# Query, key and value projections of a padded attention kernel as 64-row matmul pairs in two phases

## The chip, the cores and the metric

The kernel runs on one core of a Trainium2 chip. The metric is the device time in microseconds (us) of one execution, from its start to its end. Three executions were timed; their median is the number that a change is compared with.

## What is computed

32 sequences of up to 512 rows of 512 numbers are given with their lengths. For each sequence the rows within its length are projected to queries, keys and values of 8 heads with 64 columns each, and softmax attention over those rows is computed. Rows past the length are zero in the output.

```python
batch, max_seq, n_heads, head_dim = (32, 512, 8, 64)
for b in range(batch):
    seq_len = lengths[b]
    x_b = x[b, :seq_len].copy()
    qkv = np.matmul(x_b, w_qkv)
    q, k, v = np.split(qkv, 3, axis=-1)
    ...
    scores = scale * np.matmul(q, k.transpose(0, 2, 1))
    scores_max = np.max(scores, axis=-1, keepdims=True)
    attn = np.exp(scores - scores_max)
    attn = attn / (np.sum(attn, axis=-1, keepdims=True) + 1e-08)
    out_b = np.matmul(attn, v).transpose(1, 0, 2).reshape(seq_len, dim)
    output[b, :seq_len] = out_b
```

The lengths of this draw, sorted, are 502 447 | 446 436 | 363 357 | 351 347 | 343 333 | 323 315 | 310 261 | 260 257 | 246 230 | 223 220 | 216 183 | 164 152 | 143 140 | 134 119 | 101 86 | 79 75.

## The kernel before

A part ahead of the loops sorts the sequences by length on the chip, loads the weights and makes the projections of the longest sequence. Then the sequences are worked on in pairs, longest first. There is a loop for each width N of 512, 448, 384, 352, 320, 288, 256, 224, 192, 160, 128 and 96 columns, and a pair runs in the narrowest loop that holds it. For this draw the loops 512, 448 and 384 run once, 352 three times, 320, 288 and 256 once, 224 twice, 192 once, 160 twice, 128 and 96 once. N up to 512 and 448 means n = 4 tiles of 128 rows, 384 to 288 means n = 3, and 256 to 160 n = 2.

A loop's body has two positions, one for each sequence of the pair. A position does the attention of its own sequence and makes the projections of the next one, from `xT`, the transposed input. What it does in which order is written by hand as a string of steps in the table `ORDER`; two strings with a bar between them are for the first and the second position, one string is for both. A step is emitted on all engines that take part in it, and every engine keeps to the order of its own instructions. The steps that matter here:

- `Q0` to `Q3`, `K0` to `K3`: one 128-column block of queries or keys, 4 matmuls with 128 rows and N columns (line 261) into one PSUM bank, and a copy of the bank to `qz` or `kT` (line 1202). `V0` to `V3`: the values of one tile of rows, 4 matmuls with 128 rows and 512 columns (line 272), and a copy to `v_aug` (line 1218). A star puts the copy on ACT, else it is on DVE. `W0` makes the last values of both sequences of a pair at once (line 1109) where they fill at most half of the last tile.
- `S0`, `S1` and so on: scores. In loops of 3 and 4 tiles a step is two matmuls with 64 rows and N columns, one for each head of a pair of heads (line 1155), into two banks, and one exponential on ACT from both banks (line 1173).
- `A0` and so on: attention times values of one head (4 tiles, 16 matmuls with 65 columns) or two heads (3 tiles, 18 matmuls), line 1244, into one bank. Three DVE instructions follow: the reciprocal R of the row sums (line 1254), its product U with a mask (line 1260) and the division O into the output tile (line 1263), which frees the bank.
- `L`, `P`, `D`, `X` are the mask columns, the casts of the next input on POOL, the loads, and the transposing DMA that fills `xT` for the position after the next, which SP issues when the last projection that reads that `xT` is done.

There are 8 PSUM banks. `allotted` (line 945) gives each step the bank that has been free longest, and scores two neighbouring banks. `plan_waits` (line 36) derives from each step's reads and writes the semaphore waits of every instruction; a matmul into a bank waits for the copy, exponential or division that read it last. Between instructions of PE there is no wait.

## Time and profile before

| what | value |
| --- | --- |
| median of the runs | 338.09 us (337.75 to 338.3, 3 runs) |
| span of the profiled execution | 336.7 us |
| PE busy | 322.2 us (96%), 3832 matmuls |
| ACT busy | 264.5 us (79%) |
| DVE busy | 210.0 us (62%) |
| POOL busy | 103.6 us (31%) |

For the profiled execution only its span is known, from the first to the last instruction; the runs' median is 1.4 us above it. PE is the engine of the matmuls, PEld its weight loads, which overlap them; DVE and ACT are the two engines that read the banks; SP issues the DMAs. Matmuls are pipelined, so that the busy time of PE does not tell whether it is at its peak; the starts of successive matmuls do. In a timeline row stand the start in the span, the time from the first start to the last end, the engine, the line, the operation, its form (rows\*columns of the weights, then the moving operand) and how many instructions were merged.

### The profile page before, as it was taken

The numbers are of one execution on the slowest core, as the hardware profiler recorded it, in microseconds if no ns is written. First come the engines' busy times: TensorE is split into PE (matmuls) and PEld (weight loads), VectorE is DVE, ScalarE is ACT, GpSimd is POOL, SyncE is SP. The second block draws the span as 40 slices with busy tenths as digits, with TensorE's granted clock in tenths as the row PEclk, the third lists the DMA queues.
The fourth block names the chain that finished last, engine by engine and source line by source line (L and its number), as shares of the span: only waits on it lengthen the run. The fifth ranks groups of instructions, "written<-read, shape, count | busy, mean of one in ns | idle before, by whom it ended". The sixth has DMA issues, their size and how long they took to land.

```text
span 336.7 us, 10690 instructions
## 1 busy us (share of the span) xinstructions
PE 322.2 (96%) x3832; PEld 200.0 (59%) x3832; DVE 210.0 (62%) x654; ACT 264.5 (79%) x416; POOL 103.6 (31%) x149
## 2 busy tenths in 40 slices
PE   7999999999999999999999999999999999999881
PEld 4444545554555556556556656665677777678760
DVE  6676666666666564465455457665776656867764
ACT  5388799898978879989989988788567678777651
POOL 5546040504030320330231253043222244244321
PEclk9999999999999999999999999999999999999998
DMA  6974994484637946957947848969946966977671
GB/s 218 391 270 108 324 177 145 121 305 116 207 51 237 318 142 228 288 173 277 300 140 275 239 140 321 258 173 341 262 139 182 204 193 169 207 229 210 219 196 71
DMA packets 72124, 72.08 MB, mean 214 GB/s; under 512 B 41872, under 2 KB 41872, under 8 KB 72080
## 3 DMA queue, kind: packets, MB, share of 16 engines
q1 hardware_dynamic: 72032, 71.52, 71.9%
q8 instruction: 24, 0.39, 0.5%
q14 instruction: 20, 0.16, 0.2%
q10 hardware_dynamic: 48, 0.00, 0.0%
HBM read 28.32 MB, written 33.55 MB: 184 GB/s over the span
## 4 chain that ended last, share of the span: by engine, by line
PE 91%; DVE 3%; DMA 3%; issue 1%; SPq 0%; POOL 0%; ACT 0%; POOLq 0%
PE banks L261 38%; PE banks L272 18%; PE banks L1244 17%; PE banks L1155 16%; PE banks L1109 2%; DMA xT<-x 1%; DMA x_nat<-in_x_dram 1%; DVE out_nat L1263 1%; DVE rcp L1260 1%; PE banks L732 0%; DVE rcp L1254 0%; SPq L609 0%; DVE kT L781 0%; ACT et L1173 0%; DVE x L327 0%
## 5 line engine op out<-in xcount | busy, mean ns | idle before, releaser
L1173 ACT ACTIVATE et<-banks 128x704 f16<-128x704 f32 (+7 forms) x260 | 195.6, 826 | 31.7 <-PE banks L1155 30.3
L261 PE MATMUL banks<-xT,w_r 128*128 128x352 f16 (+11 forms) x1024 | 145.5, 287 | 1.4 <-DMA xT<-x 1.2
L332 POOL TENSOR_TENSOR x<-x_nat,mask 128x512 f16<-128x512 f32 x85 | 86.2, 1039 | 182.9 <-DVE mask L998 170.7
L261 PEld LDWEIGHTS banks<-xT,w_r 128*128 128x128 f16 x1024 | 85.4, 98 | 41.8 <-issue 7.4
L1244 PEld LDWEIGHTS banks<-v_aug,et 128*128 128x128 f16 x1792 | 66.4, 98 | 21.3 <-issue 7.2
L1244 PE MATMUL banks<-v_aug,et 128*128 128x65 f16 x1792 | 74.2, 194 | 0.7 <-ACT et L1173 0.7
L272 PE MATMUL banks<-w_r,xT 128*128 128x512 f16 x284 | 72.3, 380 | 0.6 <-DVE xT L741 0.5
L1263 DVE TENSOR_TENSOR out_nat<-banks,rcp 128x256 f32<-128x256 f32 (+1 forms) x136 | 64.1, 472 | 6.8 <-DMA out_dram<-out_nat 2.2
L1155 PE MATMUL banks<-qz,kT 64*128 64x352 f16 (+11 forms) x640 | 61.2, 298 | 2.9 <-DVE out_nat L1263 2.5
L1254 DVE RECIPROCAL rcp<-banks 128x4 f32<-128x4 f32 (+1 forms) x136 | 25.0, 184 | 44.3 <-PE banks L1244 42.8
L1202 DVE CAST qz<-banks 128x352 f16<-128x352 f32 (+5 forms) x44 | 25.3, 575 | 26.3 <-PE banks L261 25.8
L1155 PEld LDWEIGHTS banks<-qz,kT 64*128 64x128 f16 x640 | 22.6, 94 | 31.8 <-issue 23.4
L272 PEld LDWEIGHTS banks<-w_r,xT 128*128 128x128 f16 x284 | 23.7, 97 | 27.2 <-issue 5.2
L1218 DVE CAST v_aug<-banks 128x512 f16<-128x512 f32 x41 | 28.2, 692 | 16.7 <-PE banks L272 16.6
L1202 ACT CAST kT<-banks 128x352 f16<-128x352 f32 (+5 forms) x58 | 27.6, 478 | 10.2 <-PE banks L261 9.0
L1202 ACT CAST qz<-banks 128x352 f16<-128x352 f32 (+5 forms) x47 | 22.2, 477 | 6.0 <-PE banks L261 4.3
L1202 DVE CAST kT<-banks 128x512 f16<-128x512 f32 (+4 forms) x33 | 19.4, 590 | 7.3 <-PE banks L261 6.9
L1260 DVE TENSOR_TENSOR rcp<-rcp,v_aug 128x4 f32<-128x4 f32 (+1 forms) x108 | 19.6, 181 | 3.7
L1218 ACT CAST v_aug<-banks 128x512 f16<-128x512 f32 x26 | 15.6, 602 | 6.6 <-PE banks L272 6.6
L1074 DVE TENSOR_SCALAR v_aug<-alive 128x24 f16 (+3 forms) x32 | 7.7, 239 | 6.5 <-issue 6.5
L1341 POOL MEMSET kT<- 128x128 f16 (+1 forms) x8 | 1.7, 218 | 28.8 <-PE banks L1155 28.8
L418 PE MATMUL banks<-h_ones 128*128 128x128 f16 (+2 forms) x34 | 5.7, 349 | 1.9 <-POOL h_ones L408 1.9
(81 smaller groups left out, 84.0 us busy)
## 6 DMA issues: line engine op xcount, KB each, us to landing
x_nat<-in_x_dram SPq DMA_DIRECT2D x12, 768.0 KB, 5.5
out_dram<-out_nat SPq DMA_DIRECT2D x12, 768.0 KB, 4.0
x_nat<-in_x_dram SPq DMA_DIRECT2D x14, 512.0 KB, 3.8
x_nat<-in_x_dram SPq DMA_DIRECT2D x7, 1024.0 KB, 6.9
out_dram<-zeros SPq DMA_DIRECT2D x12, 512.0 KB, 5.6
out_dram<-out_nat SPq DMA_DIRECT2D x12, 512.0 KB, 4.5
out_dram<-out_nat SPq DMA_DIRECT2D x4, 1024.0 KB, 4.9
out_dram<-zeros SPq DMA_DIRECT2D x12, 256.0 KB, 5.5
```

Of the source, the lines that this page charges most:

```text
L261: last = nc.tensor.matmul(dst[:, 0:N], w_r[:, c, w0 : w0 + P], xT[:, c, 0:N], start=(c == 0), stop=(c == NC - 1),)
L272: last = nc.tensor.matmul(pv, xT[:, c, t * P : (t + 1) * P], w_r[:, c, 2 * D : 3 * D], start=(c == 0), stop=(c == NC - 1),)
L332: return engine.tensor_tensor(out=x16, in0=x32, in1=live.broadcast_to([P, D]), op=ALU.mult)
L1074: return nc.vector.tensor_scalar(out=v_bufs[o][:, t0:t1, :, HD], in0=table[:, bass.ds(at("DVE") + (j + 1), 1), t0:t1] .rearrange("p o t -> ...
L1155: last = nc.tensor.matmul(psc[par][:, x * wide : x * wide + N], kT[r, i, c0 : c0 + P], qz[r, i, 0:N], start=True, stop=True,)
L1173: return nc.scalar.activation(out=et[:, :, x0:x1, 0:N], in_=got.rearrange("p j (x q) -> p j x q", q=wide)[:, :, x0:x1, 0:N], func=AF.Exp, ...
L1202: return copy_on(act)(out=buf[:, ms, 0:N], in_=bank[:, 0 : gm * N].rearrange("p (m q) -> p m q", q=N),)
L1218: return copy_on(act)(out=v_bufs[o][:, t, :, 0:HD], in_=bank.rearrange("p (h d) -> p h d", d=HD))
L1244: last = nc.tensor.matmul(pav[:, g, qt, :], e_bufs[e][:, c0 + qt * P : c0 + (qt + 1) * P], v_aug[:, kt, h, :], start=(kt == 0), stop=(kt = ...
L1254: return nc.vector.reciprocal(out=rcp, in_=pav[:, :, :, HD])
L1260: return nc.vector.tensor_tensor(out=rcp, in0=rcp, in1=rows, op=ALU.mult)
L1263: return nc.vector.tensor_tensor(out=o_t[:, 0:n, h0 * HD : (h0 + heads) * HD].rearrange("p t (g d) -> p g t d", d=HD), in0=pav[:, :, :, 0:HD],
```

## The change

In loops of 3 and 4 tiles the steps Q, K and most of V are replaced by steps in two phases. `B0a` is the first phase and `B0b` the second of the queries' and keys' block 0; `U0a` and `U0b` are those of the values of tiles 0 and 1. A phase is four pairs of matmuls with 64 rows each, one on rows 0 to 63 and one on rows 64 to 127. In the first phase the upper rows' products go to one bank and the lower rows' to the other, in the second phase the banks are exchanged, so that both banks then hold complete sums. The second phase waits on PE's own semaphore for the last matmul of the first (`after`). The letters behind the colon say which engine copies each of the two banks, d for DVE and a for ACT. The digits behind @ give the banks of each step of these loops by hand, in place of `allotted`. All strings of these loops are new, the letters L, P, D and X included; those of the loops of 2 tiles and of 1 are the same. Some last matmuls of the A steps raise semaphores of steps that a loop doesn't have (`pads`).

```diff
@@ -31,6 +31,8 @@
     writes: tuple = ()
     dma: bool = False
     skip: bool = False
+    after: str = ""
+    pads: tuple = ()
 
 
 def plan_waits(head, bodies, entries, rare):
@@ -104,6 +106,8 @@
                     for o, is_read in needs
                     if o["by"] != op.eng or op.dma or (is_read and op.eng != "PE")
                 ]
+                if op.after:
+                    needs.append(seen[op.after][-1])
                 for o in sorted(needs, key=lambda o: -o["order"]):
                     if mine[o["by"]] >= o["count"]:
                         continue
@@ -216,28 +220,38 @@
     LOOPS = [512, 448, *range(384, 64, -32)]
 
     ORDER = {
-        512: "L P D S0 S1 S2 V2 K3 Q2 S3 S4 S5 Q3 V1 S6 K2 S7 S8 A0 S9 A1 V3* A2 S10 S11 S12 A3 K0 "
-        "Q1 A4 S13 S14 S15 V0 Q0* A5 K1* X A6 A7",
-        448: "L P D S0 S1 S2 K1 Q3 K3 S3 S4 Q2 S5 S6 V1 A0 S7 A1 S8 S9 V0 Q0 S10 S11 S12 A2 A3 V2* "
-        "A4 S13 S14 S15 K0* A5 K2* Q1 X A6 A7 | L P D S0 S1 V2 S2 S3 V1 K3 S4 S5 S6 K2 Q0 W0* S7 "
-        "S8 S9 K0 A0 Q1* A1 S10 S11 S12 A2 A3 K1* Q2 S13 S14 S15 A4 V0 A5 Q3* X A6 A7",
-        384: "L P D K1* Q1 S0 S1 S2 Q3 Q2* V1 S3 S4 V2 S5 S6 V0 A0 S7 S8 K0 Q0 S9 S10 S11 A2 K2* "
-        "A4 K3* X A6 | L P D S0 S1 S2 V0* Q0 Q3 S3 S4 S5 A0 V1 V2* S6 S7 S8 A2 K1 K3* Q1 S9 S10 "
-        "S11 A4 K2 K0 Q2* X A6",
-        352: "L P D S0 S1 S2 V0 K0* V1 S3 S4 S5 A0 V2* K1* S6 S7 S8 A2 Q2 K3* Q1* S9 S10 S11 Q0 A4 "
-        "Q3* K2* X A6",
-        320: "L P D S0 S1 S2 K0* Q2 Q1* S3 S4 S5 A0 K1 Q0* K3 S6 S7 S8 V1 V0 S9 S10 S11 A2 A4 Q3* "
-        "K2* X A6 | L P S0 S1 S2 W0* D Q1 Q2 Q3 S3 S4 S5 V1 Q0* A0 S6 S7 K2* V0 S8 S9 S10 K0 A2 A4 "
-        "S11 K3* K1 X A6",
-        288: "L P D S0 S1 V0 S2 S3 K3 K2* Q0* S4 S5 S6 A0 K1 Q2* K0 S7 S8 S9 A2 V1 S10 S11 A4 Q3* "
-        "Q1* X A6 | L P S0 S1 S2 V0 W0 D S3 S4 S5 V1 K2 Q1* K1* S6 S7 S8 A0 K0* Q0* K3* S9 S10 S11 "
-        "Q3 A2 Q2* X A4 A6",
+        512: "L P D S0@67 U1a@34 S1@01 S2@67 U1b:dd S3@12 B0a@50 S4@67 B0b:da S5@23 B3a@14 S6@67 B2a@05 S7@23 "
+        "B2b:dd S8@67 B3b:ad A0@0 S9@23 S10@67 A1@5 A2@4 A3@1 S11@23 U0a@05 S12@67 U0b:dd S13@34 A4@1 "
+        "S14@67 B1a@20 S15@45 B1b:aa A5@6 A6@5 X A7@3 | L P D S0@12 U1a@47 S1@56 U1b:da S2@12 B3a@30 "
+        "S3@45 B3b:dd S4@12 U0a@76 S5@45 U0b:dd S6@01 B1a@23 S7@45 B1b:ad S8@67 S9@01 A0@4 B2a@23 S10@67 "
+        "B2b:dd S11@45 B0a@10 S12@67 B0b:dd S13@45 S14@23 A1@6 A2@7 S15@45 A3@1 A4@3 A5@0 A6@2 X A7@5",
+        448: "L P D S0@67 B2a@32 S1@45 B2b:da S2@67 B1a@10 S3@23 B1b:dd S4@67 B0a@54 S5@23 B0b:dd S6@01 S7@67 "
+        "A0@3 V2@5 A1@4 S8@67 S9@01 A2@3 A3@2 S10@45 B3a@76 S11@01 B3b:dd S12@23 S13@45 V0@0 S14@12 "
+        "S15@67 A4@3 A5@4 V1*@1 A6@5 X A7@0 | L P S0@34 S1@67 S2@12 V1@5 W0@3 D S3@67 B2a@50 S4@12 S5@34 "
+        "B2b:dd B1a@67 S6@12 B1b:dd S7@45 B3a@03 S8@12 B3b:da S9@45 S10@67 V0@2 A0@3 S11@01 B0a@54 S12@67 "
+        "B0b:ad S13@12 A1@0 A2@3 S14@67 S15@45 A3@1 A4@0 A5@2 V2*@7 A6@1 X A7@0",
+        384: "L P D U0a@32 S0@45 S1@67 U0b:dd S2@01 B1a@54 S3@67 B1b:dd S4@23 B2a@10 S5@67 B2b:dd S6@23 S7@45 "
+        "A0@6 A2@7 S8@01 B3a@32 S9@56 B3b:aa B0a@10 S10@45 B0b:ad S11@23 V2*@6 A4@0 X A6@2 | L P D S0@67 "
+        "B3a@43 S1@01 B3b:dd S2@67 B2a@52 S3@01 B2b:dd S4@34 S5@67 V2@1 A0@2 S6@45 B1a@73 S7@01 B1b:aa "
+        "A2@2 S8@01 S9@45 U0a@67 B0a@32 S10@01 S11@45 B0b:da U0b:da A4@0 X A6@1",
+        352: "L P D V2@4 S0@56 S1@01 U0a@27 S2@56 S3@34 U0b:dd S4@01 B2a@65 S5@34 B2b:dd S6@01 A0@2 A2@7 S7@01 "
+        "B0a@56 S8@34 B0b:ad B1a@10 S9@34 B3a@27 S10@56 B1b:dd S11@34 B3b:aa A4@6 X A6@3 | L P D S0@01 "
+        "B2a@42 S1@67 B2b:da S2@01 B0a@53 S3@67 B1a@42 S4@01 B1b:dd S5@67 B0b:ad S6@01 A0@4 S7@67 U0a@25 "
+        "S8@01 S9@34 U0b:ad B3a@10 S10@67 S11@34 B3b:aa A2@5 A4@7 A6@3 V2*@6 X",
+        320: "L P D S0@45 U0a@10 S1@67 S2@45 U0b:da B1a@76 S3@45 B1b:ad S4@23 A0@0 S5@45 B0a@67 S6@23 B0b:ad "
+        "S7@45 B3a@10 S8@67 B3b:da S9@45 B2a@32 S10@67 S11@01 B2b:da A2@5 A4@4 X A6@7 | L P S0@23 S1@01 "
+        "W0@6 D B0a@32 S2@01 B0b:da S3@45 B2a@76 S4@01 S5@23 B2b:dd U0a@45 S6@01 S7@23 U0b:da B1a@76 "
+        "S8@01 B3a@32 S9@45 B1b:da B3b:dd S10@01 S11@45 A0@7 A2@6 A4@3 X A6@2",
+        288: "L P D S0@45 B2a@72 B3a@36 S1@45 B2b:da B3b:dd S2@45 S3@01 U0a@27 S4@56 S5@34 U0b:dd S6@01 B0a@56 "
+        "S7@34 B0b:da S8@12 A0@0 S9@45 B1a@37 S10@12 B1b:dd S11@45 A2@6 A4@0 X A6@1 | L P S0@23 U0a@45 "
+        "S1@67 S2@23 U0b:da S3@67 B3a@10 B2a@32 S4@45 B3b:ad B2b:dd S5@45 S6@67 W0*@1 D S7@45 B1a@32 "
+        "S8@67 B1b:dd S9@01 A0@4 A2@6 S10@01 B0a@75 S11@23 B0b:aa A4@0 X A6@1",
...
@@ -945,8 +959,12 @@
     def allotted(N):
 
 
+        todo = steps(N, 0) + steps(N, 1)
+        if "@" in ORDER[N]:
+
+            return [tuple(map(int, s.split("@")[1])) for s in todo if "@" in s]
         takes = []
-        for step in steps(N, 0) + steps(N, 1):
+        for step in todo:
             if step[0] == "S":
                 takes.append(2)
             elif step[0] in "QKVAW":
...
@@ -1137,8 +1156,8 @@
 
         def scores(g):
             group = groups[g]
-            k0 = ring.pop(0)
-            psc, W = [banks[k0], banks[k0 + 1]], len(group) * n128
+            k0, k1 = sorted(ring.pop(0))
+            psc, W = [banks[k0], banks[k1]], len(group) * n128
             i0, kt0 = group[0]
             e = i0 // pairs_per_et if n > 1 and not packed else j
             used = across * g * wide if packed else kt0 * 2 * n128
@@ -1169,7 +1188,7 @@
                     et = e_bufs[e][:, used : used + 2 * W].rearrange(
                         "p (j x q) -> p j x q", j=2, q=n128
                     )
-                got = psum[:, k0 : k0 + 2, 0 : len(group) * wide]
+                got = psum[:, k0 : k1 + 1 : k1 - k0, 0 : len(group) * wide]
                 return nc.scalar.activation(
                     out=et[:, :, x0:x1, 0:N],
                     in_=got.rearrange("p j (x q) -> p j x q", q=wide)[:, :, x0:x1, 0:N],
...
@@ -1186,8 +1205,81 @@
             if half < len(group):
                 op("S1", "ACT", lambda: exps(half, len(group)), held, (f"et{e}b",))
 
+        def halves(name, blocks, widths, copies, outs):
+
+
+
+            ks = ring.pop(0)
+
+            def matmuls(turned):
+                count = len(blocks[0])
+                for m in range(count):
+                    for c in range(NC):
+                        for half in range(2):
+                            z = half ^ turned
+                            lhs, rhs = blocks[z][m]
+                            rows = slice(HD * half, HD * (half + 1))
+                            last = nc.tensor.matmul(
+                                banks[ks[z]][:, m * widths : (m + 1) * widths],
+                                lhs(rows, c),
+                                rhs(rows, c),
+                                start=(m == 0 and c == 0 and not turned),
+                                stop=(c == NC - 1 and bool(turned)),
+                            )
+                return last
+
+            held = (f"bk{ks[0]}", f"bk{ks[1]}")
+
+            begun = ("b" if name[0] == "B" else "u") + name[1]
+
+            def first():
+                op(begun, "PE", lambda: matmuls(0), (f"xT{o}",), held)
+
+            def second(engines):
+                op(("q" if name[0] == "B" else "v") + name[1], "PE", lambda: matmuls(1), (f"xT{o}",), held, after=begun)
+                for z in range(2):
+                    by_act, bank = engines[z] == "a", banks[ks[z]]
+                    copy = lambda z=z, by_act=by_act, bank=bank: copies[z](copy_on(by_act), bank)
+                    op(outs[z][0], "ACT" if by_act else "DVE", copy, (f"bk{ks[z]}",), outs[z][1])
+
+            first()
+            return second
+
+        def half_qk(name, x):
+            ms = slice(x * gm, (x + 1) * gm)
+
+            def block(w0):
+                return lambda r, c: w_r[r, c, w0 : w0 + P], lambda r, c: xT[r, c, 0:N]
+
+            def into(buf):
+                return lambda copy, bank: copy(
+                    out=buf[:, ms, 0:N],
+                    in_=bank[:, 0 : gm * N].rearrange("p (m q) -> p m q", q=N),
+                )
+
+            blocks = [[block(part * D + (x * gm + m) * P) for m in range(gm)] for part in range(2)]
+            outs = [
+                (f"{up}{x}", tuple(f"{what}{o}.{x * gm + m}" for m in range(gm)))
+                for up, what in (("Q", "qz"), ("K", "kT"))
+            ]
+            return halves(name, blocks, N, [into(q_bufs[o]), into(k_bufs[o])], outs)
+
+        def half_values(name, x):
+            tt = (2 * x, 2 * x + 1)
+
+            def block(t):
+                return lambda r, c: xT[r, c, t * P : (t + 1) * P], lambda r, c: w_r[r, c, 2 * D : 3 * D]
+
+            def into(t):
+                return lambda copy, bank: copy(
+                    out=v_bufs[o][:, t, :, 0:HD], in_=bank.rearrange("p (h d) -> p h d", d=HD)
+                )
+
+            outs = [(f"V{t}", (f"v{o}.{t}",)) for t in tt]
+            return halves(name, [[block(t)] for t in tt], D, [into(t) for t in tt], outs)
+
         def qk(name, m0, is_q, act):
-            k = ring.pop(0)
+            (k,) = ring.pop(0)
             bank = banks[k]
             ms = slice(m0, m0 + gm)
             buf = (q_bufs if is_q else k_bufs)[o]
...
@@ -1248,6 +1340,8 @@
                                 start=(kt == 0),
                                 stop=(kt == n - 1),
                             )
+                            if here["pads"]:
+                                last.then_inc(sems[here["pads"].pop()], 1)
                 return last
 
             def reciprocal():
@@ -1286,8 +1380,17 @@
         def maybe(name, ahead, transfer):
             return transfer if n > 1 else lambda: unless_past(ahead, name, transfer)
 
+        opened = {}
         for step in steps(N, j):
+            step = step.split("@")[0]
             kind, act = step[0], step.endswith("*")
+            if kind in "BU":
+                name, engines = step[:2], step[4:]
+                if engines:
+                    opened.pop(name)(engines)
+                else:
+                    opened[name] = (half_qk if kind == "B" else half_values)(name, int(name[1]))
+                continue
             num = int(step.strip("*")[1:] or 0)
             if kind == "P":
                 op("M", "DVE", pair_mask, (), (f"m{o}",))
...
@@ -1375,6 +1481,13 @@
     head = before_loops()
     for ops in (head, *(ops for body in bodies for ops in body)):
         by_rank(ops)
+    for v in range(len(LOOPS)):
+        later = {op.name for body in bodies[v + 1 :] for op in body[0] + body[1]}
+        for ops in bodies[v]:
+            missing = {name for name in later if name[0] in "bg"} - {op.name for op in ops}
+            for op in ops:
+                if op.name == "a0":
+                    op.pads = tuple(sorted(missing))
     rare = {"Y0", "Y1", "w", "W0", "W1"}
     waits, has = plan_waits(head, bodies, entries, rare)
 
...
```

More of the change, by code (lines that the diff above doesn't have):

```diff
@@ L966, in allotted @@
                     )
-                got.append(first)
                 used = list(range(first, first + n))
+                got.append(used)
                 ages = [k for k in ages if k not in used] + used
@@ L971, in allotted @@
                 break
-        return [(k + 2) % 8 for k in got] if tiles(N) == 1 else got
+        back = 2 if tiles(N) == 1 else 0
+        return [tuple((k + back) % 8 for k in used) for used in got]
     def position(N, j, at, ring):
@@ L1213, in val @@
         def val(name, t, act):
-            k = ring.pop(0)
+            (k,) = ring.pop(0)
             bank = banks[k]
@@ L1360, in by_rank @@
             if kind:
-                op.name = f"{kinds[kind]}{left[kind]}"
+                names[op.name] = f"{kinds[kind]}{left[kind]}"
+                op.name = names[op.name]
                 left[kind] += 1
+        for op in ops:
+            op.after = names.get(op.after, "")
     here = {}
@@ L1474, in issue @@
             return instead()
+        here["pads"] = [name for name in op.pads if name in sems]
         last = op.emit()
```

11 lines of the change are left out of this document (6 added, 5 removed), and 8 rows, old and new, of the table ORDER.

## Prediction

> **What bounds the kernel now.** I read the page first: the span, the share of each engine, then the chain that ended last.
>
> ```profile
> span 336.7 us, 10690 instructions
> ...
> PE 91%; DVE 3%; DMA 3%; issue 1%; SPq 0%; POOL 0%; ACT 0%; POOLq 0%
> ...
> L1155 PEld LDWEIGHTS banks<-qz,kT 64*128 64x128 f16 x640 | 22.6, 94 | 31.8 <-issue 23.4
> ```
>
> The chain runs through PE for 91% of the span, so what PE issues, and when, is the time. An average over loops may hide a loop that another engine sets, so the second view is the table of windows, with one window for each pass of a loop. Its columns are the window, its length, then the busy time of PE, PEld, DVE, ACT and POOL.
>
> ```profile
> 121.40:145.80 24.40, 24.40 (x282) 14.33 (x284) 12.41 (x36) 21.92 (x38) 6.07 (x6) 1.00 0.81 228
> 217.20:238.80 21.60, 21.48 (x278) 13.92 (x278) 13.14 (x41) 18.31 (x36) 6.75 (x8) 1.00 0.92 265
> ```
>
> These are the first pass of loop 352 and loop 288. PE is busy for all of each but 0.12 us, at a granted clock of 1.00; ACT comes next with 21.92 of 24.40 us, DVE has a third or more to spare in both. Busy does not tell whether PE is at its peak, so the third view is PE's timeline, where a start less the start before it, divided by the matmuls between, is the price of one.
>
> ```profile
> 59.56 1.14 PE L1244 MATMUL banks<-v_aug,et 128*128 128x65 f16 x32
> 60.64 0.74 PE L1155 MATMUL banks<-qz,kT 64*128 64x448 f16 x6
> ...
> 71.73 1.03 PE L272 MATMUL banks<-w_r,xT 128*128 128x512 f16 x4
> 72.59 0.64 PE L1244 MATMUL banks<-v_aug,et 128*128 128x65 f16 x16
> 73.17 0.74 PE L1155 MATMUL banks<-qz,kT 64*128 64x448 f16 x6
> 73.84 0.93 PE L261 MATMUL banks<-xT,w_r 128*128 128x448 f16 x4
> 74.61 0.65 PE L1244 MATMUL banks<-v_aug,et 128*128 128x65 f16 x16
> 75.10 1.68 PE L261 MATMUL banks<-xT,w_r 128*128 128x448 f16 x8
> 76.61 1.14 PE L1244 MATMUL banks<-v_aug,et 128*128 128x65 f16 x32
> 77.69 0.55 PE L1155 MATMUL banks<-qz,kT 64*128 64x448 f16 x4
> 78.17 1.04 PE L272 MATMUL banks<-w_r,xT 128*128 128x512 f16 x4
> ...
> 94.31 1.14 PE L1244 MATMUL banks<-v_aug,et 128*128 128x65 f16 x32
> 95.45 1.46 PE L261 MATMUL banks<-xT,w_r 128*128 128x384 f16 x8
> ```
>
> From 128-row work to 128-row work nothing is lost: four 512-column matmuls take 72.59 - 71.73 = 0.86 us (0.215 each), eight 448-column ones 1.51 (0.189 each), 16 matmuls of an A step 0.49 (0.0306 each). From 128 to 64 rows 76.61 to 77.69 is 1.08 us for 32 matmuls that make 0.98: 0.10 lost. From 64 to 128 rows 73.17 to 73.84 is 0.67 for three pairs. At 0.189 a pair that is 0.57, and again 0.10 is lost. So two 64-row matmuls run side by side in the time of one 128-row matmul of the same width, and every run of 64-row work between 128-row work costs about 0.205 us for its way in and out. PE loses hardly anything else in these loops, so the change has to be judged by what it takes from PE and by which waits of PE it makes.
>
> **What it removes: changes of row mode.** I count the runs of 64-row steps in the strings, over both positions and round the loop. Before, only S has 64 rows: 14, 13, 9, 8, 9 and 9 runs in loops 512, 448, 384, 352, 320 and 288. After, S, B and U are of one kind, and only A, V and W interrupt them: 7, 8, 5, 4, 4 and 5. With 352 passed three times the sum falls from 78 to 41. 37 x 0.205 = 7.6 us come off PE. The projections themselves cost what they did: a phase of four pairs takes four slots, two phases make two blocks, as eight 128-row matmuls do.
>
> [...]
>
> **What it adds: the wait between the phases.** The second phase waits for the end of the first on PE itself. What the wait costs follows from a matmul's length and from how fast a waiter starts. Lengths by form:
>
> ```profile
> L1155 PE MATMUL banks<-qz,kT 64*128 64x352 f16 x144 | 14.9, 312 | 0.0
> L1155 PE MATMUL banks<-qz,kT 64*128 64x512 f16 x64 | 9.5, 381 | 0.4 <-DVE kT L781 0.4
> L1155 PE MATMUL banks<-qz,kT 64*128 64x448 f16 x64 | 8.3, 353 | 0.0
> L1155 PE MATMUL banks<-qz,kT 64*128 64x384 f16 x48 | 5.5, 326 | 0.0
> L1155 PE MATMUL banks<-qz,kT 64*128 64x320 f16 x48 | 4.8, 300 | 0.0
> L1155 PE MATMUL banks<-qz,kT 64*128 64x288 f16 x48 | 4.5, 286 | 0.0
> ```
>
> And the timeline at the entry of loop 512, where PE and ACT stood waiting:
>
> ```profile
> 21.34 1.29 DVE L781 CAST kT<-banks 128x512 f16<-128x512 f32 x2 [0.34 <-PE banks L261]
> 22.08 0.99 PE L1155 MATMUL banks<-qz,kT 64*128 64x512 f16 x6 [0.35 <-DVE kT L781]
> 22.52 1.94 ACT L1173 ACTIVATE et<-banks 128x1024 f16<-128x1024 f32 x2 [0.76 <-PE banks L1155]
> 22.68 0.10 PEld L1155 LDWEIGHTS banks<-qz,kT 64*128 64x128 f16 x2 [0.48 <-DVE kT L781]
> ```
>
> DVE ends at 22.63 and PE starts at 22.68; a matmul from 22.08 ends at 22.46, and ACT starts at 22.52. A waiter starts 0.05 to 0.06 us after the end. Nearly always one S step, one pair, stands between the phases. The second phase then starts late by the length of the last matmul, plus 0.06, less two slots: 0.381 + 0.06 - 0.43 = 0.01 us at 512, 0.035 at 448, 0.06 at 384, 0.075 at 352, 0.09 at 320, 0.10 at 288. Where two S steps or another phase stand between, nothing is left. Single-S places are 10, 7, 7, 3 x 4, 4 and 4. With 0.01 for the first pair after a stop that gives 0.2 + 0.3 + 0.5 + 1.0 + 0.4 + 0.4 = 2.8 us. The end that speaks for the change is 0; at the other, each of the 44 places shows a weight load of 0.094 as well, 4.1 us more. I take 2.8, because PE at 22.68 started with its weight load and lost no load's length. Queued behind each such wait are PE's own next S and A steps, and ACT, which waits for those.
>
> **What it moves: banks at the entry of a loop.** The strings name their banks, and three loops begin on a bank that the last A step of the loop before still holds until DVE's division. I lay DVE beside PE from these rows (R at 60.25 and 61.01 are back to back, so are those at 214.74 and 215.64):
>
> ```profile
> 60.25 0.18 DVE L1254 RECIPROCAL rcp<-banks 128x4 f32<-128x4 f32 x1 [0.50 <-PE banks L1244]
> 60.67 0.42 DVE L1263 TENSOR_TENSOR out_nat<-banks,rcp 128x256 f32<-128x256 f32 x1
> 61.01 0.17 DVE L1254 RECIPROCAL rcp<-banks 128x4 f32<-128x4 f32 x1
> 214.74 0.20 DVE L1254 RECIPROCAL rcp<-banks 128x6 f32<-128x6 f32 x1
> 215.17 0.56 DVE L1263 TENSOR_TENSOR out_nat<-banks,rcp 128x384 f32<-128x384 f32 x1
> 215.64 0.19 DVE L1254 RECIPROCAL rcp<-banks 128x6 f32<-128x6 f32 x1
> L1202 DVE CAST kT<-banks 128x320 f16<-128x320 f32 x6 | 2.9, 490 | 1.5 <-PE banks L261 1.4
> xT<-x SPq DMA_TRANSPOSE x78, 3.0
> ```
>
> DVE needs 0.76 us for an A step of 4 tiles and 0.90 for one of 3; PE makes them in 0.49 and 18 x 0.0306 = 0.55. Where A steps stand together, DVE falls behind.
>
> Loop 512 ends B0b:dd S13 S14 A1 A2 S15 A3 A4 A5 A6@2 A7, and 448 begins S0 B2a@32. From the end of B0b's issue, PE has two S (0.43), a switch (0.10), two A (0.98), an S between two switches (0.42), five A (2.45), a switch and a 448 pair (0.29): B2a could start at 4.67. DVE makes B0b's two copies from 0.21 for 1.29, takes up A1 at 1.45, is at A6 five chains later, 5.25, and ends its division 0.84 after that, at 6.09; PE sees it at 6.14. Stall 1.5 us. Loop 320 ends B3b:dd S10 S11 A0 A2 A4 A6@2, and 288 begins S0 B2a@72: PE is there at 0.27 + 0.10 + 2.20 + 0.24 = 2.81. DVE's two copies of 0.49 are over when A0's sums are there at 1.1, A6 follows at 3.8 and is divided at 4.8. Stall 2.0. Loop 384 ends U0b:da A4 A6@1, and 352 begins V2 S0 S1@01: 2.31 on PE against 2.81 on DVE, 0.5. Together 4.0 us; behind each stand all of PE's next steps and the exponentials that ACT would make of them. Bounds: 1.0 if DVE lags no further than before, and 5 if it lags one copy of 0.49 more at both large places.
>
> Smaller ones. The first S@67 of loop 512 takes bank 7, whose copy ends at 22.63, while before two S pairs were issued ahead of that wait: 0.43. Its S2@67 follows S0@67 after 0.22 + 0.86 + 0.22 = 1.30 us, while S0's exponential is done at 0.44 + 0.97 (half of 1.94) + 0.05 = 1.46: 0.2. The same wait in 320 and some below 0.1 I put at 0.6. The first instruction of a loop gathers more semaphores than before. At 95.45, with two, the entry cost 1.14 - 0.98 = 0.16; at 60.64, with one, none: 0.3 in all, an estimate. X moves by one A step at most. Its transposes land 3.0 us after issue and are read a position later, 10 us or more, and SP issues them ahead of the same store, so they cost nothing; with that cover gone a late one would cost PE its delay. Copies move from ACT to DVE in 352 (14 to 9 on ACT), where ACT was the fuller one: no cost beyond the entry waits above. Raising semaphores on A matmuls adds no instruction.
>
> Sum: -7.6 + 2.8 + 4.0 + 0.4 + 0.2 + 0.6 + 0.3 = +0.7 us, so a span of 337.4. The median of the runs stood 1.4 above the profiled span, which makes 338.8; I round up to 338.9, as each small wait pushes later exponentials back.
>
> **The rivals.** *The entries cost little* (the other side: faster). If DVE comes to those A steps level with PE, B2a finds its bank nearly free, and of 4.0 us 1.0 remains: 335.8. It decides at DVE's lag behind PE when 448 is entered: below 1.3 us, as at 60.64 (O would end at 61.01 + 0.84 = 61.85), against the 2.4 worked out. For it speaks that a copy or chain a little shorter counts five times over; against it that seven A steps make 5.3 us of DVE work in 3.9 us of PE. Chance 0.22.
>
> *The phase wait shows the weight load* (slower): 2.8 becomes 6.9, and 343.0. For it: nothing after the wait can be loaded early; against it the start at 22.68. Chance 0.13.
>
> *Pairs that accumulate cannot load ahead* (slower): 0.094 for each of 640 pairs, 399. Only S is evidence against it, and S does not accumulate. Chance 0.02. [...]
>
> *The mode switches do not go*, because S and B pairs drain in between as well: 338.8 + 7.6 = 346.4. The pairs at 73.17 speak against it. Chance 0.03.
>
> **How the numbers follow.** The forecast has 0.60, with an own range of 337.3 to 340.4 (self-waits and small terms by 1.5 either way); below 0.2%, 0.7 us, a measurement of this kernel can hardly tell it from no change. Of its 0.60, 0.36 lies over 338.8, 0.18 within 0.7 of 338.1 and 0.06 under. The first rival gives 0.20 to faster and 0.02 to same, the other three 0.18 to slower. That makes 0.26 faster, 0.20 same, 0.54 slower. The range reaches down over the first rival to 335.4 and up to 341.2, and leaves out the slow rivals.
>
> **What would show it.** Right: no 128-row row of projections except V and W between 64-row rows in the PE timeline of 448; gaps of 0.05 to 0.1 us before second phases in 352 and 288; PE waiting for out_nat (line of the division) about 1.5 us near 61 and 2 us near 217. Wrong: no such waits in PE's list, or one of the phase waits over 0.15 us, or a pair's slot longer than 0.215 us at 512 columns.

## The result and the profile after

The changed kernel took **339.64 us** (median of 20 runs, 338.64 to 341.56), the kernel before 338.15 (20 runs, 337.56 to 339.69) beside it: ratio 1.0048, 95% interval 1.0033 to 1.0063. It is slower by 0.5%; the forecast was 338.9, range 335.4 to 341.2, with slower as the likeliest. The 20 times lie in two groups of ten, 338.64 to 339.36 and 339.93 to 341.56; "lower" and "upper group" below mean these, and the median lies in the gap between them. The profiled execution, 340.88 us, is of the upper group, and in it PE's clock falls to half at the entry of loop 288. For the other executions only the mean granted clock is known: 0.989 to 0.992 in nine of the upper group, 0.992 to 0.997 in the lower (3.4 us at half clock take 0.005 off the mean). By that the half clock sets the upper group apart, but for its lowest time: 339.93 has 0.995, and why it is high is not known.

The top of its page, the chain, and those of PE's waits in which the change shows:

```profile
span 339.0 us, 12004 instructions
...
PE 87%; DVE 5%; DMA 2%; issue 2%; ACT 1%; SPq 0%; POOL 0%; DVEq 0%; ACTq 0%; POOLq 0%
...
PE banks L1222 <- DVE out_nat L1357: 3.0, 2, 1.8
...
PE banks L1174 <- DVE out_nat L1357: 1.4, 2, 1.1
...
PE banks L1174 <- DVE kT L795: 1.0, 1, 1.0
PE banks L1174 <- DVE v_aug L1310: 0.7, 1, 0.7
```

L1222 is the 64-row halves (B and U), L1174 the scores, L1357 the division, L795 a copy ahead of the loops. DVE has risen in the chain from 3 to 5%. PE waits 3.0 us for divisions at two halves; before, it waited for divisions only in the loops of one and two tiles at the end. Of the 1.4 us at scores, 1.1 is such a wait that both kernels have, in loop 128, and 0.3 is new, at the entry of 352. The wait for L795's copy, at the entry of 512, was 0.35 before. Where the 2.3 us of span went is read from one window for each loop (columns as before: PE, PEld, DVE, ACT, POOL, then the granted clock), of after and then of before:

```profile
22.80:60.20 37.40, 37.36 (x512) 19.40 (x513) 21.28 (x62) 33.88 (x38) 12.83 (x14) 1.00 0.72 196
60.20:96.02 35.82, 34.37 (x478) 18.95 (x478) 24.28 (x78) 30.28 (x38) 9.28 (x11) 1.00 0.50 166
96.02:121.42 25.40, 25.40 (x361) 14.62 (x361) 14.75 (x42) 21.86 (x32) 6.28 (x7) 1.00 0.80 231
121.42:194.52 73.10, 72.09 (x1084) 43.25 (x1080) 43.44 (x125) 60.67 (x98) 18.96 (x20) 1.00 0.76 227
194.52:217.13 22.61, 22.41 (x357) 14.75 (x357) 13.69 (x41) 19.48 (x34) 7.03 (x9) 1.00 0.80 229
217.13:241.90 24.77, 22.95 (x357) 15.41 (x358) 15.49 (x49) 17.31 (x31) 6.76 (x8) 0.93 0.91 274
241.90:339.00 97.10, 87.07 (x1216) 66.60 (x1216) 65.80 (x238) 65.43 (x105) 31.99 (x39) 0.98 0.63 182
```

```profile
22.08:60.64 38.56, 38.56 (x418) 19.42 (x418) 24.90 (x67) 33.47 (x38) 12.93 (x14) 1.00 0.68 188
60.64:95.45 34.81, 34.81 (x415) 18.83 (x413) 23.06 (x72) 30.30 (x39) 9.26 (x11) 1.00 0.57 181
95.45:121.37 25.92, 25.92 (x280) 14.19 (x281) 15.80 (x43) 21.24 (x32) 6.27 (x7) 1.00 0.83 227
121.37:194.59 73.22, 73.21 (x842) 42.91 (x842) 37.69 (x108) 65.75 (x114) 18.42 (x19) 1.00 0.74 227
194.59:217.23 22.64, 22.64 (x277) 14.05 (x277) 15.14 (x43) 18.62 (x33) 7.47 (x10) 1.00 0.80 241
217.23:238.79 21.56, 21.45 (x276) 13.88 (x277) 13.13 (x40) 18.31 (x36) 6.75 (x8) 1.00 0.92 265
238.79:336.70 97.91, 86.96 (x1216) 66.53 (x1216) 65.60 (x238) 65.40 (x105) 31.98 (x39) 0.99 0.69 188
```

Loops 512 and 384 gain (1.2 and 0.5 us), 352 and 320 gain next to nothing, 448 loses 1.0 and 288 loses 3.2, at a mean clock of 0.93. The part ahead of 512 is 0.7 longer, the part behind 288 0.8 shorter. PE's timeline in after, at the two entries that were forecast and at the one that was not:

```profile
60.20 0.36 PE L1174 MATMUL banks<-qz,kT 64*128 64x448 f16 x2
61.80 0.93 PE L1222 MATMUL banks<-xT,w_r 64*128 64x448 f16 x8 [1.23 <-DVE out_nat L1357]
...
124.00 0.31 PE L1174 MATMUL banks<-qz,kT 64*128 64x352 f16 x2
125.05 0.32 PE L1174 MATMUL banks<-qz,kT 64*128 64x352 f16 x2 [0.74 <-DVE v_aug L1310]
...
217.13 0.30 PE L1174 MATMUL banks<-qz,kT 64*128 64x288 f16 x2
219.24 2.10 PE L1222 MATMUL banks<-xT,w_r 64*128 64x288 f16 x16 [1.81 <-DVE out_nat L1357]
221.11 0.47 PE L1174 MATMUL banks<-qz,kT 64*128 64x288 f16 x2
...
222.96 0.42 PE L1174 MATMUL banks<-qz,kT 64*128 64x288 f16 x4
```

From the start of the one pair of scores, B2a waits until 1.60 us (448) and 2.11 us (288) later; less the pair's slot of 0.19 and 0.12, that is 1.41 and 1.98 us lost. Behind the second, 16 matmuls take from 219.24 to 221.11, 0.234 a pair, where 288 columns cost 0.123 at the full clock. The windows show the clock:

```profile
215.80:219.20 3.40, 1.52 (x43) 1.22 (x39) 3.05 (x11) 0.78 (x2) 0.00 (x0) 1.00 0.94 280
219.20:222.60 3.40, 3.36 (x30) 2.48 (x32) 0.50 (x4) 0.67 (x2) 1.61 (x2) 0.50 1.21 283
```

### The profile page after: what moved, and what is told of

Same layout as the page of the kernel before. It is cut to its first block, busy times and chain, and to the rows that moved or that the text cites. A ratio compares the mean times of both kernels' runs of the same rounds, so it can differ in the third digit from the quotient of the medians.

```text
span 339.0 us, 12004 instructions
## 1 busy us (share of the span) xinstructions
PE 320.6 (95%) x4472; PEld 203.4 (60%) x4472; DVE 213.8 (63%) x675; ACT 260.4 (77%) x395; POOL 103.8 (31%) x149
## 4 chain that ended last, share of the span: by engine, by line
PE 87%; DVE 5%; DMA 2%; issue 2%; ACT 1%; SPq 0%; POOL 0%; DVEq 0%; ACTq 0%; POOLq 0%
PE banks L1222 33%; PE banks L1336 15%; PE banks L1174 14%; PE banks L275 13%; PE banks L286 9%; DVE out_nat L1357 2%; PE banks L1128 2%; DMA x_nat<-in_x_dram 1%; DMA xT<-x 1%; DVE rcp L1354 1%; DVE rcp L1348 1%; PE banks L746 0%; ACT et L1192 0%; DVE kT L795 0%; SPq L623 0%
## 5 line engine op out<-in xcount | busy, mean ns | idle before, releaser
L1222 PE MATMUL banks<-xT,w_r 64*128 64x352 f16 (+5 forms) x1024 | 102.5, 324 | 3.0 <-DVE out_nat L1357 3.0
L1174 PE MATMUL banks<-qz,kT 64*128 64x352 f16 (+11 forms) x640 | 76.5, 297 | 4.5 <-DVE out_nat L1357 1.4
L1222 PEld LDWEIGHTS banks<-xT,w_r 64*128 64x128 f16 x1024 | 47.1, 95 | 40.7 <-PE banks L1222 10.4
L1357 DVE TENSOR_TENSOR out_nat<-banks,rcp 128x256 f32<-128x256 f32 (+1 forms) x136 | 64.1, 471 | 5.4 <-DMA out_dram<-out_nat 0.8
L275 PE MATMUL banks<-xT,w_r 128*128 128x160 f16 (+6 forms) x512 | 51.4, 252 | 0.8 <-DMA xT<-x 0.5
L1174 PEld LDWEIGHTS banks<-qz,kT 64*128 64x128 f16 x640 | 27.6, 94 | 30.8 <-issue 8.0
L275 PEld LDWEIGHTS banks<-xT,w_r 128*128 128x128 f16 x512 | 39.5, 98 | 7.4 <-issue 1.5
L286 PE MATMUL banks<-w_r,xT 128*128 128x512 f16 x156 | 39.3, 379 | 0.5 <-DVE xT L755 0.5
L1222 PE MATMUL banks<-w_r,xT 64*128 64x512 f16 x256 | 33.0, 376 | 0.2 <-issue 0.2
L1274 DVE CAST v_aug<-banks 128x512 f16<-128x512 f32 x24 | 15.9, 690 | 17.5 <-PE banks L1222 17.5
L1255 DVE CAST kT<-banks 128x352 f16<-128x352 f32 (+5 forms) x41 | 22.1, 548 | 7.0 <-PE banks L1222 7.0
L1222 PEld LDWEIGHTS banks<-w_r,xT 64*128 64x128 f16 x256 | 12.2, 94 | 10.6 <-PE banks L1222 1.0
```

Of the source, the lines that this page charges most:

```text
L275: last = nc.tensor.matmul(dst[:, 0:N], w_r[:, c, w0 : w0 + P], xT[:, c, 0:N], start=(c == 0), stop=(c == NC - 1),)
L286: last = nc.tensor.matmul(pv, xT[:, c, t * P : (t + 1) * P], w_r[:, c, 2 * D : 3 * D], start=(c == 0), stop=(c == NC - 1),)
L1174: last = nc.tensor.matmul(psc[par][:, x * wide : x * wide + N], kT[r, i, c0 : c0 + P], qz[r, i, 0:N], start=True, stop=True,)
L1222: last = nc.tensor.matmul(banks[ks[z]][:, m * widths : (m + 1) * widths], lhs(rows, c), rhs(rows, c), start=(m == 0 and c == 0 and not tur ...
L1255: return lambda copy, bank: copy(out=buf[:, ms, 0:N], in_=bank[:, 0 : gm * N].rearrange("p (m q) -> p m q", q=N),)
L1274: return lambda copy, bank: copy(out=v_bufs[o][:, t, :, 0:HD], in_=bank.rearrange("p (h d) -> p h d", d=HD))
```

## The experiments

The theory going in: what the change saves in row modes is lost again in waits for DVE's divisions at the entries of 448, 352 and 288, and the half clock follows from the last of these. The rival: the two-phase form itself (row modes that do not go, longer phase waits) is the loss.

**The row mode's price.** Blocks of 128 rows in the same order and banks; no phase wait; 168 runs of 64-row work instead of 41:

```diff
-                            rows = slice(HD * half, HD * (half + 1))
...
+                        lhs, rhs = blocks[turned][m]
+                        last = nc.tensor.matmul(
+                            banks[ks[turned]][:, m * widths : (m + 1) * widths],
+                            lhs(slice(0, P), c), rhs(slice(0, P), c),
+                            start=(c == 0), stop=(c == NC - 1))
```

> The steps, banks and copies of the changed kernel, but each phase makes one whole block with four 128-row matmuls, and there is no wait between phases. Runs of 64-row work rise from 41 to 168. Theory (a run costs 0.205 us, the phase waits 2.8 in all): 127 x 0.205 - 2.8 = +23.2 us, about 362.5, some less where a switch falls into a wait that stands anyhow. Rival (the pairs themselves are slower than 128-row matmuls when they accumulate, so that going back to 128 rows gains on each): well under +20.

Measured: 364.39 us (5 runs, 362.54 to 364.47), ratio 1.0745 (1.0724 to 1.0765). Its timeline in 448, with a pair of scores between 128-row blocks of four:

```profile
66.70 0.36 PE L1174 MATMUL banks<-qz,kT 64*128 64x448 f16 x2
67.00 0.93 PE L1218 MATMUL banks<-xT,w_r 128*128 128x448 f16 x4
67.86 0.36 PE L1174 MATMUL banks<-qz,kT 64*128 64x448 f16 x2
```

0.30 for a slot of 0.189 and 0.86 for four: 0.11 in and 0.10 out, 0.21 a run. Its span of 362.4 stands 23.4 over after's 339.0, and both have the half clock at the entry of 288 (here from 239.63 to 243.04, mean granted clock of the run 0.991). With the 2.8 of phase waits that go, 26.2 us fall to 127 runs, 0.206 each, the price worked out before. So the saving is real, and the rival that row modes stay falls.

**The phase wait.** In loop 384 the seven single score steps between two phases are moved behind the second (`U0a S1 U0b` becomes `U0a U0b S1`):

> In loop 384 the S step between the two phases is moved behind the second in seven places. Theory (the second phase waits for the end of the first's last matmul, length + 0.06 us, and S covers one slot of it): each of the seven gaps becomes 0.326 + 0.06 - 0.162 = 0.225 us instead of 0.066, and S comes later for ACT, which costs some 2 us more in waits of A and S steps for exponentials: +3 to +4 us, 342.5. Rival (the wait costs a weight load more, which S hid): gaps of 0.32.

Measured: 344.21 us (one run), span 342.4. Two phases in a row, then after's form with one pair between:

```profile
98.16 1.71 PE L1222 MATMUL banks<-xT,w_r 64*128 64x384 f16 x16
99.71 0.49 PE L1174 MATMUL banks<-qz,kT 64*128 64x384 f16 x4
```

```profile
100.59 0.33 PE L1174 MATMUL banks<-qz,kT 64*128 64x384 f16 x2
100.82 0.82 PE L1222 MATMUL banks<-xT,w_r 64*128 64x384 f16 x8
```

Eight slots of 0.1625 make 1.30 of the 1.55: 0.25 lost without cover (0.225 expected). With one pair between, 0.23 for a slot of 0.1625: 0.07 lost (0.06 forecast). That is near the 0.22 which a matmul's length of 0.326 and the 0.06 of a waiter's start leave over a slot of 0.1625; with a weight load of 0.094 on top it would be 0.32. The loop went from 25.4 to 29.1 us, though seven times 0.18 is 1.3; most of the rest is PE waiting for exponentials that come late (0.58, 0.58 and 0.86 us). This profile has the half clock at 288 too (mean granted clock 0.991); without its 1.6 us the run stands at 342.6, as expected.

**The entry of 288, by less work for DVE.** Loop 320's second position divides only 32 of each 64 columns, so the output there is left half undone:

```diff
-                    in0=pav[:, :, :, 0:HD],
+                    in0=pav[:, :, :, 0:wid],   # wid = HD // 2 in 320, j == 1
```

> Left out: in the second position of loop 320 the division O makes only the first 32 of each head's 64 columns. It is one DVE instruction of 0.56 us that becomes about 0.36. Theory (288's first B step waits for DVE's chain R, U, O, four A steps long): each link is 0.2 shorter, so that wait falls from 1.98 to about 1.2 us, PE's idle time falls under what lets the clock down, and the upper group of times goes: median 338.3. Rival (the wait is set by the loop's entry itself, its branch and code, or by a DMA): wait and median as in the changed kernel, 339.6.

Measured: 338.45 us (12 runs, 337.91 to 339.21), ratio 0.9999 (0.9989 to 1.0009). The wait is 1.19, the clock stays whole (1.00 from 219.20 to 222.60), and the upper group is gone:

```profile
217.74 0.30 PE L1174 MATMUL banks<-qz,kT 64*128 64x288 f16 x2
219.05 1.16 PE L1222 MATMUL banks<-xT,w_r 64*128 64x288 f16 x16 [1.01 <-DVE out_nat L1358]
...
221.13 0.42 PE L1174 MATMUL banks<-qz,kT 64*128 64x288 f16 x4
```

The wait is 0.79 shorter, and four divisions of 0.36 instead of 0.56 us make 0.8. The lag of DVE sets the wait, as the theory has it.

**The half clock, by work in the gap.** First try, with the filler behind the first scores (`S0@45 F@01 B2a@72`):

> At the entry of loop 288 the changed kernel's PE stands idle for 2.0 us, and in its profile the granted clock is 0.5 for 3.41 us right after, in which 14 pairs run at 0.24 instead of 0.123 us. This kernel issues 9 pairs of 512 columns (9 x 0.216 = 1.94 us) into banks 0 and 1 in that gap, with results that nobody reads; everything else is the same. Theory (the wait on DVE's division and the clock are two costs): the wait for the bank still ends at the same time, so the 2.0 us stay, but the clock stays at 1.0, and the upper half of the changed kernel's times (339.9 to 341.6) goes: median 339.0 (338.6 to 339.4), 0.6 below the changed kernel's 339.6. Rival (the times' two groups come from elsewhere, an entry of another loop or the tail): they stay, median 339.6 or, with the filler in the way, more.

A miss: 341.92 us (341.55 to 342.7), ratio 1.0105 (1.0089 to 1.0121). The filler waited for the same divisions and came on top:

```profile
219.47 2.12 PE L1430 MATMUL banks<-w_r 64*128 64x512 f16 x18 [1.72 <-DVE out_nat L1357]
```

So it told nothing of the cause, but its profile shows idle time of 1.72 us (1.81 in after) that was not followed by half clock: behind it eight pairs of 288 columns take from 221.43 to 222.41, 0.123 each. Second try, the filler ahead of the scores (`F@45 S0@45 B2a@72`):

> Nine pairs of 512 columns whose result is not used (9 x 0.215 = 1.94 us of PE, into banks 4 and 5) stand ahead of S0@45 in loop 288's first string; that string is unrolled for one position and run once. Theory: the 2.0 us at the entry of 288 are idle time of PE that waits for the division of loop 320's last A step on DVE, and the half clock after it is an answer to PE standing idle. Then the filler takes the idle time: the wait at 219 shrinks to 0.1 us or less, the granted clock stays 1.0 behind it, the times form one group at 339.0 and the upper group (339.9 and more) is gone. Rival: the half clock has another cause (its place in the run, the draw of power): then the upper group stays, with a median near 339.6. Second rival: the wait isn't DVE's lag but comes at a fixed distance behind PE's own work; then the filler comes on top of it, 340.9.

Measured: 339.56 us (11 runs, 338.78 to 340.12), ratio 1.0024 (1.0012 to 1.0036); the kernel before stood at 338.59 beside it, 0.4 above the first comparison.

```profile
217.75 2.12 PE L1430 MATMUL banks<-w_r 64*128 64x512 f16 x18
219.69 0.30 PE L1174 MATMUL banks<-qz,kT 64*128 64x288 f16 x2
```

1.94 us of added work cost nothing: it lies in the gap. Its own times fall in one group, 1.0 above the kernel before, as the lower group is (0.9). With PE busy the half clock did not come: eight pairs behind the scores take from 219.86 to 220.83, 0.121 each, and the mean granted clock is 0.995, against 0.989 in after. So in these runs it went with the idle time, and the place in the run alone did not bring it. Why only some runs have it, by the author's estimate, stands in the last section.

**The entry of 352.** V2's copy goes from DVE to ACT (`V2@4` becomes `V2*@4` in 352's first string):

> In loop 352's first string the copy of V2's bank goes to ACT instead of DVE, in all three passes; nothing else. Theory: the 0.90 us that S3@34 waits in the first pass is bank 4, which V2's copy on DVE holds, late because DVE comes 1.15 us late into the loop. Then S3's wait falls from 0.90 to under 0.1. ACT makes the copy (about 0.55 us) ahead of S0's exponential, so S2@56, which needs S0's banks, may wait up to 0.3 us in each of three passes. Sum between -0.9 and 0: 338.6 (338.1 to 339.0) in the lower group. Rival: S3 waits for S0's or S1's exponential on ACT; then its wait grows to about 1.4 us and the time by 0.5, 339.5.

Measured: 338.75 us (10 runs), ratio 1.0012 (0.9996 to 1.0028); six, from 338.33 to 338.75, make the lower group, four lie from 340.11 up. The six stand 0.1 under the kernel before, where after's lower group stands 0.9 over it. The 0.90 is gone:

```profile
124.02 0.46 PE L1174 MATMUL banks<-qz,kT 64*128 64x352 f16 x4
124.32 1.03 PE L1222 MATMUL banks<-w_r,xT 64*128 64x512 f16 x8
```

S3 now follows S2 at once. In the two later passes S2 waits some 0.2 us each, as forecast. S3 had waited for DVE, which in after comes late to that loop without waiting for anything:

```profile
122.36 0.56 DVE L1357 TENSOR_TENSOR out_nat<-banks,rcp 128x384 f32<-128x384 f32 x1
124.07 0.26 DVE L1093 TENSOR_SCALAR v_aug<-alive 128x24 f16 x1 [1.15 <-issue]
```

**The old strings in 320 and 288.** These two loops take the strings of the kernel before, the loops ahead of them keep the new ones.

> Loops 320 and 288 take their strings of the kernel before (128-row projections, banks dealt by age), the loops ahead of them keep the new ones. Theory: what the change loses lies at the entry of 288. Against the lower group of the changed kernel, 339.0: the 2.0 us wait at 288 goes, the phase waits of both loops (0.8) and the wait of S2 in 320 (0.25) go, and 5 + 4 row-mode changes at 0.205 come back (1.85): -1.2, so 337.8, and up to 0.8 more where the old string's S0 and S1 now meet banks that loop 352's last A steps hold. So 338.1 (337.7 to 338.6), no half clock at 219 and no upper group, and loop 288 at 21.6 us instead of 24.8. Rival: the phase waits and the entries of 448 and 352 are the loss; then only 0.8 goes, 1.85 comes back, 340.0.

A miss: 340.63 us (5 runs, 339.98 to 340.81), ratio 1.0049 (1.0035 to 1.0062). No half clock at 219 (twelve matmuls of 288 columns from 220.30 take 1.64 us), no second group, but slower than the sum by 2.5, of which 0.4 lies in the comparison (the kernel before at 338.59). Three things, read from its profile:

```profile
195.87 0.45 PE L1170 MATMUL banks<-qz,kT 64*128 64x320 f16 x4 [0.59 <-DVE out_nat L1353]
...
225.44 0.30 PE L1170 MATMUL banks<-qz,kT 64*128 64x288 f16 x2 [0.37 <-DVE kT L1290]
```

```profile
220.71 0.20 DVE L1089 TENSOR_SCALAR v_aug<-alive 128x16 f16 x1 [1.33 <-issue]
...
330.75 0.42 DVE L1353 TENSOR_TENSOR out_nat<-banks,rcp 128x256 f32<-128x256 f32 x1 [1.61 <-DMA out_dram<-out_nat]
```

The old string of 320 meets 352's last A steps (0.59, inside the 0.8 allowed). In 288 DVE comes 1.33 us late from the entry, where it lost 0.33 in the kernel before, and its copies hold up scores: the loop, from 218.62 to 240.90, takes 22.3 us and not 21.6. In the last loops DVE waits 1.61 us for a store to free its output buffer, and the stretch from 240.90 to the end is 1.0 longer than in after. The first belongs to the theory. The second is no backlog of divisions but a pause of DVE, and it comes here with the very strings with which it was 0.33 before; so what lengthens it is not in the strings of these two loops, and it stays open. The third has nothing to do with the strings that were changed; the kernel before has such a wait too, of 1.36 us, and after one of 0.24, and why the stores fall so is open.

**The order of the A steps.** If DVE's backlog is the matter, A steps that stand farther apart take it away. First only in 512's second string:

```diff
-        "... B0b:dd S13@45 S14@23 A1@6 A2@7 S15@45 A3@1 A4@3 A5@0 A6@2 X A7@5"
+        "... B0b:da S13@45 A3@3 A4@6 S14@01 A2@7 S15@45 A1@6 A5@3 A6@4 X A7@1"
```

> Only the second string of loop 512 is reordered: of the six A steps at its end two move between S13 and S14 (A3 A4 S14 A2 S15 A1 A5 A6 A7), B0b's second copy goes to ACT, and the banks are dealt so that the bank pair 32, which B2a takes first in loop 448, was last held by A3 and A2 and by no late A step. One run of 64-row work more (42 for 41, 0.2 us). Theory: B2a's 1.41 us at the entry of 448 is DVE's backlog of divisions, so it falls to 0.3 or less; waits inside 512's second string rise by 0.2 to 0.4. Sum -0.8: a lower group at 338.2 (337.9 to 338.6), an upper group as before about 1.7 above it, since 288's entry is untouched. Rival: DVE has the same work whatever its order, and the backlog shows at S14 or S15 instead: lower group at 339.0 or above.

Measured: 339.44 us (12 runs, 337.93 to 340.04), ratio 1.0020 (1.0004 to 1.0036), span 338.0; half clock still there (0.51 from 218.60 to 222.00).

```profile
60.75 0.37 PE L1174 MATMUL banks<-qz,kT 64*128 64x448 f16 x2
60.94 0.93 PE L1222 MATMUL banks<-xT,w_r 64*128 64x448 f16 x8
```

The wait of 1.41 is gone (0.19 is the slot), and 448 takes 34.5 us instead of 35.8. The edit does three things: it spreads the A steps, gives B0b's second copy to ACT, and lets B2a's bank hang on A5's division instead of A6's. The rows of DVE divide the gain: A6's division ended 1.45 us behind the loop's first scores in after and ends 0.75 behind them here, and A5's ends as they start. So about half is less backlog, by the spread or the copy, which no run parts, and half is the choice of the bank. Then in the second strings of 512, 384 and 320, with copies moved to ACT there and in 352, and two small moves in 320's first string:

> The same in the second strings of 512, 384 and 320 (A steps spread, last ones on banks that the next loop takes late, one or two copies moved to ACT); 44 runs of 64-row work for 41 (0.6 us). Theory: the waits at the entries of 448 (1.41), of 352 (0.45, S1) and of 288 (1.98) fall to 0.3 or less each, the half clock at 219 and the upper group go with the last, and new waits of 0.2 at 512 and 384 and up to 0.9 at the first U of 320 come. -3.8 + 0.8 + 0.6 + 0.4 + 0.9 = -1.1 against the lower group of 339.0, so 337.9 (337.0 to 338.4), one group. Rival: the backlog only moves: 339.0 or above.

Measured: 337.95 us (12 runs, 337.33 to 338.51), one group; ratio 0.9988 (0.9975 to 1.0001), against 337.9 expected. Its largest new waits were U0a's 0.69 in 320 and 0.66 in 288, the second behind a late DVE (1.47 us at the entry). Hence the last:

```diff
-        320: "L P D S0@45 U0a@10 S1@67 ..."    288: "... S1@45 B2b:da B3b:dd ..."
+        320: "L P D S0@45 U0a@20 S1@67 ..."    288: "... S1@45 B2b:aa B3b:da ..."
```

> The strings of e9 with two edits. In 320 the first value phase takes banks 2 and 0 (U0a@20) instead of 1 and 0, of which bank 1 is held by A6's division: its wait of 0.69 us falls to 0.3 or less. In 288's first string B2b's second copy goes to ACT too and B3b's first (aa and da for da and dd), because DVE stands idle for 1.47 us at that loop's entry while ACT is free: the 0.66 us that U0a waits for B2's copy falls to 0.3 or less. Theory: -0.75 against e9, whose median was 0.12% under the kernel before; so ratio 0.9966 (0.995 to 0.998), about 337.2 where the kernel before takes 338.3. Rival: DVE's idle time at the entry of 288 only hides work that it must still do, and the wait moves to the next reader of its copies (S or U behind): 337.9, ratio 0.9988.

Measured: **337.14 us** (12 runs, 336.51 to 338.18), ratio 0.9959 (0.9939 to 0.9980) to the kernel before: a version that beats both. In 288 the wait is 0.27, in 320 still 0.6, now for ACT's copy of a value block:

```profile
span 334.7 us, 11999 instructions
...
193.61 1.04 PE L1222 MATMUL banks<-w_r,xT 64*128 64x512 f16 x8 [0.44 <-ACT v_aug L1310]
...
218.59 0.41 PE L1174 MATMUL banks<-qz,kT 64*128 64x288 f16 x4
219.11 1.04 PE L1222 MATMUL banks<-w_r,xT 64*128 64x512 f16 x8
```

## Why the prediction was right, and where its steps were off

The sign, and the mechanism that set it, were right; by stages (us, after less before; the prediction's 0.9 of small waits and entry semaphores had no place):

| Stage | Prediction's terms | Sum | Measured |
|---|---|---|---|
| ahead of 512 | S0@67 | +0.4 | +0.7 |
| 512 | -1.4 modes, 0.2 phases, 0.2 S2 | -1.0 | -1.2 |
| 448 | -1.0, 0.3, entry 1.5 | +0.8 | +1.0 |
| 384 | -0.8, 0.5 | -0.3 | -0.5 |
| 352 | -2.5, 1.0, entry 0.5 | -1.0 | -0.1 |
| 320 | -1.0, 0.4 | -0.6 | 0.0 |
| 288 | -0.8, 0.4, entry 2.0 | +1.6 | +3.2 |
| to the end | none | 0 | -0.8 |

- *The number.* That the sum meets the lower group (0.8 over the kernel before forecast, 0.9 measured) is in part luck. By the table, the part ahead of 512 and loops 448, 352 and 320 came out 2.0 us worse than their terms, 512, 384 and the end 1.2 better, and the 0.9 without a place made up the rest.
- *Row modes, 7.6 us.* Right: 0.206 a run where 128-row blocks bring them back.
- *Phase waits, 2.8 us.* Right: 0.07 at 384, and 0.25 without cover. The rival with a visible weight load falls, as does the one in which accumulating pairs load late: in after, four such pairs with new weights each take 0.49 us at 288 columns (225.37 to 225.86), which is their slots and no more.
- *Entries of 448 and 288, 1.5 and 2.0.* Measured 1.41 and 1.98. The second shrinks by 0.79 when DVE's divisions are shorter, and both go when the A steps are spread and the banks dealt anew. The rival "the entries cost little" falls by the same rows.
- *"No cost beyond the entry waits above"* for the copies that go from ACT to DVE in 352 failed. S3 lost 0.90 there. DVE's 1.20 us pause at the entry stands in the trace before too, at 123.61, and cost PE nothing there (busy for 24.40 of 24.40 us in that pass). What covered it was not named, and it went.
- *Behind the entry wait, only what is queued.* The prediction priced the 2.0 us as idle time and left out the clock of 0.50 behind it: from 219.24 to 222.96 the profiled run takes 3.72 us for work that the half-division kernel does in 2.08 (219.05 to 221.13). These 1.6 us come in about half the runs, and are the gap between the lower group, about 339.0, where the forecast lay, and the upper.
- *320 and the end.* In 320 S2's wait, 0.26, is among the 0.9 without a place; the rest of the 0.6 was not traced. The -0.8 at the end was not foreseen: PE's wait for the last transposes fell from 1.2 to 0.5 us; the strings there are unchanged, and why the transposes land earlier was not traced. The +0.7 ahead of 512 is the forecast wait of S0@67, with 0.4 put on it.

## What to carry to other kernels

Here the 7.6 us saved on PE were lost again, 1.41 and 1.98 of them in waits at two loop entries where DVE was behind with its divisions; so lay the engine that reads PE's banks beside PE at each loop's end before counting the gain. Where A-like steps that one engine must finish are bunched ahead of a loop, spread them and let the next loop begin on the banks freed first; here that, with some copies moved to ACT, turned 0.5% slower into 0.4% faster. Look at the granted clock behind a long PE wait: the 1.98 us at the entry of 288 cost 1.6 us more in about half the runs.

## What the runs showed of the hardware that was not expected

PE's clock fell to half for 3.41 us at a wait of 2.0 us, in about half the runs. Five traces have it, and in each it starts a whole number of times 3.41 us ahead of the half clock with which the run ends: 34 times, 116.05 us, in four (in after at 219.21 and 335.26), 35 times in the run with 128-row blocks. It does not start where the wait ends: in two of them PE had been at work again for 1.0 and 1.2 us (with V2's copy by ACT from 218.84, and the half clock at 220.06). The author's reading of these times, which no run put to the test by itself, is that the clock goes by steps of 3.41 us which don't start with the wait, and that what counts is how much of the wait falls into one of them. With the steps laid from the end of each run, the step that holds most of the wait, and the clock in the next:

| Run | Step (us) | PE busy in it (of 3.41 us) | Clock in the next step |
|---|---|---|---|
| after, at 288 | 215.80 to 219.21 | 1.52 | 0.50 |
| phases in a row in 384 | 220.43 to 223.84 | 1.49 | 0.50 |
| blocks of 128 rows | 236.22 to 239.63 | 1.51 | 0.50 |
| V2's copy by ACT | 216.65 to 220.06 | 1.52 | 0.50 |
| A steps spread in 512 | 215.11 to 218.52 | 1.50 | 0.50 |
| filler behind the scores | 215.95 to 219.36 | 1.69 | 1.00 |
| half division, a wait of 1.19 | 217.64 to 221.05 | 2.30 | 1.00 |
| after, at 448, a wait of 1.41 | 58.78 to 62.19 | 2.18 | 1.00 |

The five steps in which PE was busy for 1.49 to 1.52 us were followed by half clock, those with 1.69, 2.18 and 2.30 were not. A wait of 1.98 us that lies wholly in one step leaves PE at most 1.43 of 3.41 us; so, by that reading, about 1.5 us comes about only where nearly all of the wait falls into one step, which would account for the half clock in only some of the runs. That is an estimate from these eight rows.

DVE stood for 0.3 to 1.5 us at the entries of loops with nothing in the profile to wait for (1.15 us at 352; at 288 0.33 before, 1.33 after, 1.47 in the spread version). No run here shows the cause, and why the pause at 288 grew with the new code, and stayed long with the old strings of 320 and 288 in it, stays open. What is shown is that urgent copies were better placed on ACT there: S3's 0.90 us at 352 went with V2's copy, and U0a's 0.66 at 288 fell to 0.27 with B2's and B3's.
